# A two-layer encoder trunk on one NeuronCore: operands of the inner groups of hidden columns split one product sooner, the order at the end of the channel mixer changed, the last 256 hidden columns turned by VectorE and DMA, two constant tiles made in place

## The chip, the cores and the metric

The kernel runs on one core of one Trainium2 chip. The metric is the device time of one execution in microseconds. Before the change it was 931.45 us, the median of three runs (931.14, 931.45 and 932.04 us).

## The reference, cut to what matters

Two layers over 256 tokens of width 1024. Each layer runs a SwiGLU channel mixer with half weight, an attention block (a windowed and a differential head group), and a second SwiGLU mixer; a last RMSNorm follows. All of it is float32. The change touches the channel mixer, which runs four times, and the constants of the attention.

```python
D_MODEL, SEQ, DEPTH, D_FF = 1024, 256, 2, 2816

def swiglu(h, w_gate, w_up, w_down):
    return (jax.nn.silu(h @ w_gate) * (h @ w_up)) @ w_down

for l in range(DEPTH):
    x = x + 0.5 * swiglu(rms_norm(x, ffn1_norm[l]), ffn1_w_gate[l], ffn1_w_up[l], ffn1_w_down[l])
    x = x + attention_block(x, l)        # uses lam = exp(sum(lam_q1*lam_k1)) - exp(sum(lam_q2*lam_k2)) + lam_init
    x = x + 0.5 * swiglu(rms_norm(x, ffn2_norm[l]), ffn2_w_gate[l], ffn2_w_up[l], ffn2_w_down[l])
return rms_norm(x, final_norm)
```

## The kernel before, in words

**Products.** A float32 product is made of three TensorE matmuls on a faster float32 form: each operand is split into a high part (a rounding copy by ScalarE) and a low part (a subtraction by VectorE), and high x high, low x high and high x low are accumulated in PSUM. For weights this splitting is `emit_split` (L205): one ACT `CAST w<-raw` and one DVE `TENSOR_TENSOR w<-raw,w` for each half of a 1 MB weight tile. `weights()` (L262) is called ahead of every product; through `ahead` (L241) it first writes down the splits, and the loads that SyncE issues, of the products that come next, up to six halves further on. 14 `w` buffers (seven halves) and 6 `raw` buffers hold them, so the split of a half waits until TensorE has let go of the half seven places before.

**Groups.** The 2816 hidden columns are five groups of 512 (0 to 4) and a last group of 256. Groups 0, 1 and 3 are plain: gate and up, four products of 24 matmuls each (`Plain`, L691). Groups 2 and 4 use a seven-product scheme over the two token tiles and the two halves of the depth (`Seven`, L642): parts a, d, ab, c, abc, bc, abcd with 12 matmuls each; its weight sums are partly made by accumulating DMAs on GpSimd's queue (`gather`, L154), and `abcd` is the last part of a group. The last 256 columns have gate and up side by side in one tile and take two products of 24 matmuls (`last`, first and second half of the depth).

**Turning.** The hidden values come out with tokens on the partitions; the down projection needs the hidden columns there. For groups 0 to 4 `Flip` (L719) does this without TensorE: two DVE stream transposes (32x32 blocks) into one buffer, then eight DMAs on SyncE's queue (L727) that carry the blocks to their partitions. `Flip.operands` (L729), called at "turned" in the order, splits the result into high and low parts: two ACT casts and two DVE subtractions on `s` tiles (`s<-s`). For the last 256 columns `turn` (L707) uses four TensorE transposes with the identity and one split out of PSUM.

**Order.** `order()` (L34) is a list by hand, walked in `ffn` (L763), and each engine executes its instructions in the order in which they are written down. "flip" starts group 1's or 3's `Flip` (groups 0, 2 and 4 start it on their own when their last product is done), "turned" splits its result, "down" g, h is group g's share of the output columns h (24 matmuls, written d0_0 to d4_1 below). "aside" is `attention_constants` (L517) in the first mixer. After the list, `ffn` splits group 4's operands (L785) and computes the last group's hidden values (L786); `ffn_end` (L792) runs three quarters of d4_0, calls the deferred `turn` (L806), and then the last quarter. `tail` multiplies the last 256 columns.

In the second half of one mixer the order before is, for TensorE: ... abc, 3, bc, 3, abcd, 3, 3 (parts of group 2 and products of group 3 in turn), a, d1_0, d, d1_1, ab, d2_0, c, d2_1, abc, last 0, bc, d3_0, abcd, last 1, d3_1, d4_0 with the transposes in it, then d4_1 and the tail.

**Buffers.** The `s4` pool has 14 buffers of 4 KB per partition for operands, hidden values and flips. Two of them hold constants from the start of the kernel until "aside" in the first mixer: `dist_i` (an iota) and `lams` (the four lambda vectors and their products).

Of the kernel before, what the change touches and what calls it, by code (L numbers as in the profile page):

```python
# [9 lines left out]
F32 = mybir.dt.float32  # L10
F32R = mybir.dt.float32r
AF = mybir.ActivationFunctionType
ALU = mybir.AluOpType

P = 128
D = 1024
S = 256
DEPTH = 2
# [3 lines left out]
NGRP = FF // 512  # L22
# [11 lines left out]
def order():  # L34

    two, four = [[("seven", g, p) for p in ("a", "d", "ab", "c", "abc", "bc", "abcd")] for g in (2, 4)]
    one, three = [[("plain", g, (w, k0)) for w in range(2) for k0 in (0, 4)] for g in (1, 3)]
    downs = [[("down", g, h) for h in range(2)] for g in range(4)]
    last = [("last", 0, k0) for k0 in (0, 4)]
    sums = [("sums", 0, 1)]  # L40
    turn = [[("turned", g, 0)] for g in range(4)]
    flip = [[("flip", g, 0)] for g in range(4)]
    aside = [("aside", 0, 0)]

    def weave(a, b):
        out = []
        for i in range(max(len(a), len(b))):
            out += a[i:i + 1] + b[i:i + 1]
        return out

    seq = sums + one[:1] + sums + two[:1] + sums + one[1:2] + sums + two[1:2] + turn[0] + one[2:]
    seq += two[2:3] + flip[1] + downs[0][:1] + two[3:4] + downs[0][1:]
    seq += weave(two[4:], three) + flip[3] + turn[1]
    seq += four[:1] + downs[1][:1] + four[1:2] + turn[2] + downs[1][1:] + four[2:3] + downs[2][:1] + four[3:4] + turn[3] + downs[2][1:] + four[4:5]
    seq += last[:1] + four[5:6] + downs[3][:1] + four[6:] + last[1:] + aside + downs[3][1:]
    return seq


# [5 lines left out]
def trunk(ctx: ExitStack, tc: tile.TileContext, x, n1, g1, u1, d1, nm, w_in, sink,  # L64
# [4 lines left out]
    class Kept:  # L69


        def __init__(self, eng):
            self.eng = eng
# [26 lines left out]
    def bank():  # L100
        return ps.tile([P, 512], F32, tag="ps", bufs=8, name=nm_("ps"))

    def halves(b):
        return b.rearrange("p (a n) -> p a n", a=2)

    def blk(dt=F32R):
        return s4.tile([P, 2, 512], dt, tag="s4", name=nm_("s4"))
# [379 lines left out]
    slopeB = [2.0 ** -(2 * (h + 1)) for h in range(4)]  # L487
    lam_init = [0.8 - 0.6 * math.exp(-0.3 * l) for l in range(DEPTH)]

    dist_i = s4.tile([P, 2, S], mybir.dt.int32, tag="s4", name="dist_i")  # L490
    lams = blk(F32)
    lin = lams[:, 0].rearrange("p (i d) -> p i d", i=4)
    lpr = lams[:, 1, 0:2 * DEPTH * 64].rearrange("p (i d) -> p i d", i=2)
    def constants():
        for i, g in enumerate((nm, n2)):
            pool.dma_start(grow[i * 16:(i + 1) * 16], g.rearrange("l (k p) -> (l k) p", p=P))
        pool.dma_start(grow[32:34], subln)
        pool.dma_start(snk_in, sink.rearrange("l h -> (l h)").partition_broadcast(P))
        for i, a in enumerate((lq1, lk1, lq2, lk2)):
            pool.dma_start(lin[:, i], a.rearrange("l d -> (l d)").partition_broadcast(P))  # L500
        pool.iota(dist_i.rearrange("p a b -> p (a b)"), pattern=[[P, 2], [-1, S]], base=0, channel_multiplier=1)

        for c in range(4):
            pool.memset(qscA[0:64, c:c + 1], -0.125 / slopeA[c])
            pool.memset(qscA[64:128, c:c + 1], -0.125 / slopeA[c + 4])
            pool.memset(qscB[:, c:c + 1], -0.125 / slopeB[c])

        sv = snk_in.rearrange("p (l s c) -> p l c s", l=DEPTH, s=2)
        for t in range(2):
            for l in range(DEPTH):  # L510
                pool.tensor_copy(snk[:, l, :, t, :], sv[:, l])
        pool.tensor_scalar(nsnk.rearrange("p a b c d -> p (a b c d)"), snk.rearrange("p a b c d -> p (a b c d)"),
                           -1.0, 0.0, op0=ALU.mult, op1=ALU.add)
        for i in range(2):
            pool.tensor_tensor(lpr[:, i], lin[:, 2 * i], lin[:, 2 * i + 1], op=ALU.mult)

    def attention_constants():  # L517
        gsl = bank()
        pe.transpose(gsl[:, 0:NG - 16], grow, ident[:NG - 16, :NG - 16])
        dve.tensor_copy(gcol[:, 16:NG], gsl[:, 0:NG - 16])  # L520
        dflat = distB.rearrange("p a b -> p (a b)")
        aflat = distA.rearrange("p a b -> p (a b)")
        dve.tensor_copy(aflat, dist_i.rearrange("p a b -> p (a b)"))
        dve.scalar_tensor_tensor(dflat, in0=aflat, scalar=-1.0, in1=aflat, op0=ALU.mult, op1=ALU.max)
        dve.tensor_scalar(aflat, dflat, 128.5, BIG, op0=ALU.is_gt, op1=ALU.mult)
        dve.tensor_tensor(aflat, aflat, dflat, op=ALU.add)
        dve.tensor_reduce(lsum.rearrange("p a b -> p (a b)"),
                          lpr.rearrange("p a (l d) -> p (a l) d", l=DEPTH), axis=mybir.AxisListType.X, op=ALU.add)
        lex = const.tile([P, 2, DEPTH], F32, name="lex")
        act.activation(lex, lsum, AF.Exp)  # L530
        dve.tensor_tensor(nlam, lex[:, 1], lex[:, 0], op=ALU.subtract)
        for l in range(DEPTH):
            dve.tensor_scalar_add(nlam[:, l:l + 1], nlam[:, l:l + 1], -lam_init[l])
            dve.tensor_scalar_mul(gsub[:, l:l + 1], gcol[:, 48 + l:49 + l], 1.0 - lam_init[l])
# [13 lines left out]
    def split(dst, src, scale=None):  # L548

        act.copy(dst[:, :, 0:S], src)  # L550
        dve.tensor_tensor(dst[:, :, S:512], src, f(dst[:, :, 0:S]), op=ALU.subtract)
# [57 lines left out]
    def ffn(norm, aside=None, before=None, final=False):  # L609
# [4 lines left out]
        def gate(gs):  # L614
            g = []
            for t in range(2):
                n = gs[t].shape[1]
                g.append(silu(tmp().rearrange("p a n -> p (a n)")[:, :n], gs[t], t))
            return g
# [5 lines left out]
        def hidden(g, us):  # L625
            h = blk(F32)
            for t in range(2):
                up(h, us[t], g[t], t)
            return h
# [12 lines left out]
        class Seven:  # L642


            def __init__(self, g):
                self.g = g
# [57 lines left out]
                    hid[self.g] = hidden(self.gate, self.acc)  # L704
                    self.gate = self.acc = None

        def turn(hs, n):  # L707
            out_ = []
            for i in range(n):
                sl = halves(bank())  # L710
                for c in range(2):
                    for t in range(2):
                        pe.transpose(sl[:, c, t * P:(t + 1) * P], hs[:, t, (2 * i + c) * P:(2 * i + c + 1) * P], ident)
                hb = blk()
                split(hb, sl)
                out_.append(hb)
            return out_

        class Flip:  # L719


            def __init__(self, h):
                sq, self.back = blk(F32), blk(F32)
                for t in range(2):
                    dve.transpose(sq[:, t].rearrange("p (g m) -> p g m", g=4), h[:, t].rearrange("p (c i g) -> p g c i", c=4, g=4))
                    for b in range(4):
                        sp.dma_start(self.back[:, t, b * P:(b + 1) * P], sq[32 * b:32 * b + 32, t])  # L727

            def operands(self):  # L729

                out_ = []
                for i in range(2):
                    hb = blk()
                    src = self.back.rearrange("p t (b c j) -> p c (t b) j", b=4, c=4)[:, 2 * i:2 * i + 2]
                    hi, lo = [hb[:, :, a:a + S].rearrange("p c (y j) -> p c y j", j=32) for a in (0, S)]
                    act.copy(hi, src)
                    dve.tensor_tensor(lo, src, f(hi), op=ALU.subtract)
                    out_.append(hb)
                return out_
# [23 lines left out]
        for what, n, part in ORDER:  # L763
# [17 lines left out]
            elif what == "last":  # L781
                if part == 0:
                    gu = [bank(), bank()]
                tokens(gu, norm.xs, weights(), part)
        hT = hid.pop(NGRP - 1).operands()  # L785
        h = hidden(gate([b[:, 0:256] for b in gu]), [b[:, 256:512] for b in gu])  # L786
        return accs, hT, lambda: turn(h, 1)

    BY_TOKENS = [(k, t) for t in range(2) for k in range(2)]
    G4 = 4 * (NGRP - 1)  # L790
# [1 line left out]
    def ffn_end(parts, last):  # L792

        accs, hT, rest = parts
        hT = [None] * (2 * (NGRP - 1)) + hT
        hE = []
        w = {0: weights()}

        def group(h, order, a=None, c=slice(None), first=0):
            tokens(a or accs[h], hT, w[h], G4, first=first, last=last[h], order=order, cols=c)  # L800

        def tail(h, order=BY_TOKENS, a=None, c=slice(None)):
            tokens(a or accs[h], [None] * (2 * NGRP) + hE, w["rest"], 4 * NGRP, last=last[h], order=order, cols=c, h=h)

        group(0, [(k, t) for k in range(3) for t in range(2)])
        hE.extend(rest())  # L806
        group(0, [(3, t) for t in range(2)])
        w["rest"] = weights()
        w[1] = weights(2)
        return group, tail  # L810
# [337 lines left out]
```

## Time and profile before

| quantity | value |
|---|---|
| median of three runs | 931.45 us |
| the profiled execution, device time | 930.48 us |
| its span, first to last instruction | 928.7 us |
| TensorE matmuls busy | 914.0 us, 98% of the span |
| VectorE busy | 708.2 us, 76% |
| ScalarE busy | 558.7 us, 60% |
| GpSimd busy | 52.7 us, 6% |
| granted TensorE clock, mean | 0.999 |
| DMA | 205.10 MB, mean 221 GB/s |

A row of the timeline reads: start in us, duration in us, engine, line, operation, output and inputs, form, number of merged instructions, and in brackets the idle time of the engine before it with what ended that. PE is TensorE, DVE is VectorE, ACT is ScalarE, POOL is GpSimd, SPq is SyncE's queue. The program's tiles are `w` (split weights), `raw` (weights as loaded), `s` (the `s4` pool), `q` and `v` (sums for the seven-product scheme), `ps` (PSUM). Most instructions carry L79, the line of a recording helper, so they are told apart by their tiles and their place in time. Matmuls overlap, so the duration of a row is longer than the distance from its start to the next row's start; the pace of TensorE is read from starts.

### The profile page before, as it was taken

How to read it: one execution, taken by the hardware profiler on the slowest of the kernel's cores; microseconds unless marked ns; L12 is line 12 of the kernel's file. 1: busy time of each engine (PE TensorE's matmuls, PEld its weight loads, DVE VectorE, ACT ScalarE, POOL GpSimd, SP SyncE). 2: the span in 40 equal slices, each digit the busy share in tenths (PEclk: the TensorE clock that was granted, in tenths of full speed). 3: DMA queues.
4: the chain of work that ended last, by engine and by line, in shares of the span. 5: the costliest groups of instructions: out<-in, count | busy, mean ns of one | idle time of the engine just before them, and what ended most of it. 6: DMA issues, size and time to landing. Idle time of an engine off the chain costs nothing.

```text
span 928.7 us, 12908 instructions
## 1 busy us (share of the span) xinstructions
PE 914.0 (98%) x4684; PEld 772.4 (83%) x4684; DVE 708.2 (76%) x998; ACT 558.7 (60%) x869; POOL 52.7 (6%) x73
## 2 busy tenths in 40 slices
PE   8999999999999999999999999999999999999997
PEld 6878788799898888788888887888999888887886
DVE  6688987778956788887668978876796658978873
ACT  7665665567735665565475655555685475656552
POOL 0400010000000000010000100000000000100001
PEclk9999999999999999999999999999999999999999
DMA  9979999645424879999648899986642448899921
GB/s 339 307 214 335 298 251 330 187 174 140 137 90 135 249 197 324 261 253 306 211 170 245 217 312 244 291 272 198 180 150 91 135 140 246 213 317 262 274 92 46
DMA packets 133936, 205.10 MB, mean 221 GB/s; under 512 B 6126, under 2 KB 54320, under 8 KB 133872
## 3 DMA queue, kind: packets, MB, share of 16 engines
q1 hardware_dynamic: 119856, 177.76, 57.9%
q0 software_dynamic: 12928, 25.46, 16.0%
q10 hardware_dynamic: 1088, 1.05, 0.4%
q8 instruction: 37, 0.61, 0.3%
q14 instruction: 27, 0.22, 0.1%
HBM read 192.71 MB, written 1.05 MB: 209 GB/s over the span
## 4 chain that ended last, share of the span: by engine, by line
PE 91%; SPq 2%; DVE 2%; DMA 1%; issue 1%; ACT 1%; ACTq 0%; POOLq 0%; POOL 0%; DVEq 0%
PE ps L79 91%; SPq L727 2%; DVE s L79 1%; DMA s<-s 1%; ACT w L79 1%; DVE w L79 1%; DMA xk<-in_x_dram 0%; ACT tmp L79 0%; ACT s L79 0%; DVE xk L79 0%; DVE tmp L79 0%; ACTq L79 0%; POOLq L1143 0%; POOL rf L79 0%; DVE rf L79 0%
## 5 line engine op out<-in xcount | busy, mean ns | idle before, releaser
L79 PE MATMUL ps<-w,s 128*128 128x512 f32 (+1 forms) x2994 | 692.6, 390 | 4.1 <-DVE s L79 3.1
L79 PEld LDWEIGHTS ps<-w,s 128*128 128x128 f32 x2994 | 557.1, 188 | 123.2 <-DVE s L79 6.1
L79 DVE TENSOR_TENSOR w<-raw,w 128x1024 fp32r<-128x1024 f32 (+1 forms) x416 | 437.4, 1088 | 121.9 <-ACT w L79 118.6
L79 ACT CAST w<-raw 128x1024 fp32r<-128x1024 f32 (+1 forms) x416 | 377.9, 943 | 220.6 <-PE ps L79 151.6
L79 PE MATMUL ps<-s,w 128*128 128x256 f32 x672 | 84.0, 285 | 0.0
L79 PEld LDWEIGHTS ps<-s,w 128*128 128x128 f32 x672 | 81.7, 192 | 1.1
L79 PE MATMUL ps<-w,q 128*128 128x512 f32 x288 | 69.2, 389 | 0.0
L79 PEld LDWEIGHTS ps<-w,q 128*128 128x128 f32 x288 | 54.1, 188 | 11.2
L79 ACT ACTIVATE s<-ps,gcol 128x256 fp32r<-128x256 f32 (+1 forms) x80 | 31.3, 477 | 20.6 <-PE ps L79 20.6
L79 DVE STREAM_TRANSPOSE s<-s 128x512 f32<-128x512 f32 x40 | 41.5, 1075 | 0.0
L79 POOL DMA_DIRECT2D raw<-in_ffn_w_up_dram x16 | 20.7, 1297 | 297.0 <-DVE w L79 126.2
L79 ACT ACTIVATE s<-s,negm 128x256 f32<-128x256 f32 x64 | 31.9, 500 | 6.5 <-DVE negm L79 6.5
L79 ACT CAST q<-tmp 128x512 fp32r<-128x512 f32 x20 | 12.4, 620 | 38.8 <-DVE tmp L79 38.8
L79 DVE TENSOR_TENSOR s<-s,s 128x512 fp32r<-128x512 f32 x40 | 25.7, 683 | 10.7 <-ACT s L79 10.7
L79 DVE SCALAR_TENSOR_TENSOR s<-ps,gcol,s 128x256 fp32r<-128x256 f32 x48 | 20.3, 478 | 14.4 <-ACT s L79 14.3
L79 ACT ACTIVATE tmp<-ps,r 128x512 f32<-128x512 f32 (+1 forms) x40 | 24.3, 641 | 6.4 <-PE ps L79 5.8
L79 ACT CAST s<-s 128x512 fp32r<-128x512 f32 x40 | 22.6, 613 | 1.4 <-DMA s<-s 1.4
L79 PE MATMUL ps<-w,v 128*128 128x512 f32 x96 | 23.1, 389 | 0.0
L79 POOL TENSOR_TENSOR r<-ms,mhalf 128x2 f32<-128x2 f32 x6 | 4.3, 710 | 300.6 <-DVE ms L79 300.6
L79 DVE TENSOR_TENSOR tmp<-tmp,ps 128x512 f32<-128x512 f32 x24 | 16.5, 686 | 6.3 <-PE ps L79 6.3
L79 PEld LDWEIGHTS ps<-w,v 128*128 128x128 f32 x96 | 18.0, 188 | 3.7
L79 DVE SCALAR_TENSOR_TENSOR s<-ps,hr,tmp 128x512 f32<-128x512 f32 (+1 forms) x32 | 20.5, 679 | 0.2 <-ACT tmp L79 0.2
(110 smaller groups left out, 427.7 us busy)
## 6 DMA issues: line engine op xcount, KB each, us to landing
raw<-in_ffn_w_down_dram SPq DMA_DIRECT2D x44, 1024.0 KB, 7.3
raw<-in_ffn_w_gate_dram SPq DMA_DIRECT2D x39, 1024.0 KB, 6.0
raw<-in_ffn_w_up_dram SPq DMA_DIRECT2D x39, 1024.0 KB, 5.4
raw<-in_ffn_w_up_dram POOLq DMA_DIRECT2D x16, 1024.0 KB, 8.8
raw<-in_w_in_dram SPq DMA_DIRECT2D x14, 1024.0 KB, 5.5
s<-s SPq DMA_DIRECT2D x160, 64.0 KB, 4.3
raw<-in_ffn_w_gate_dram POOLq DMA_DIRECT2D x8, 1024.0 KB, 11.8
raw<-in_ffn_w_gate_dram SPq DMA_DIRECT2D x8, 512.0 KB, 6.3
```

The lines of the kernel that those rows point to most:

```text
L79: ins = issue(*a, **k)
L727: sp.dma_start(self.back[:, t, b * P:(b + 1) * P], sq[32 * b:32 * b + 32, t])
```

## The change

The order list gets two more "turned" entries (groups 4 and 5) and is rearranged. Group 1's operands are split behind the second product of group 3, three products sooner; group 2's ahead of part d, one product sooner; group 3's behind abc. Then come d2_1, bc, last 0, abcd, last 1, "aside", d3_0, group 4's split, d3_1 and the split of the last 256 columns. So d3_0 moves from between bc and abcd to behind last 1, abc moves ahead of d2_1, and all of d3 stands between the last hidden product and d4. `Flip` takes a width; the last 256 columns (called group 5) go through it as soon as their second product is done: two DVE transposes of 256 columns and eight DMAs in place of four TensorE transposes. `turn` is gone. `dist_i` becomes a view of `distA` and the lambda vectors a view of `distB`, so the two `s4` buffers are free; the sum of the lambda products is taken ahead of the distances that overwrite it.

```diff
-    turn = [[("turned", g, 0)] for g in range(4)]
+    turn = [[("turned", g, 0)] for g in range(6)]
...
-    seq += weave(two[4:], three) + flip[3] + turn[1]
-    seq += four[:1] + downs[1][:1] + four[1:2] + turn[2] + downs[1][1:] + four[2:3] + downs[2][:1] + four[3:4] + turn[3] + downs[2][1:] + four[4:5]
-    seq += last[:1] + four[5:6] + downs[3][:1] + four[6:] + last[1:] + aside + downs[3][1:]
+    seq += weave(two[4:6], three[:2]) + turn[1] + two[6:] + three[2:] + flip[3]
+    seq += four[:1] + downs[1][:1] + turn[2] + four[1:2] + downs[1][1:] + four[2:3] + downs[2][:1] + four[3:5] + turn[3] + downs[2][1:]
+    seq += four[5:6] + last[:1] + four[6:] + last[1:] + aside + downs[3][:1] + turn[4] + downs[3][1:] + turn[5]
...
-    dist_i = s4.tile([P, 2, S], mybir.dt.int32, tag="s4", name="dist_i")
-    lams = blk(F32)
-    lin = lams[:, 0].rearrange("p (i d) -> p i d", i=4)
-    lpr = lams[:, 1, 0:2 * DEPTH * 64].rearrange("p (i d) -> p i d", i=2)
+    dist_i = distA.bitcast(mybir.dt.int32)
+    lin = distB.rearrange("p a (i d) -> p (a i) d", d=DEPTH * 64)
+    lpr = lin.rearrange("p (a i) d -> p a i d", i=2)[:, :, 0]
...
-            pool.tensor_tensor(lpr[:, i], lin[:, 2 * i], lin[:, 2 * i + 1], op=ALU.mult)
+            pool.tensor_tensor(lpr[:, i], lpr[:, i], lin[:, 2 * i + 1], op=ALU.mult)
...
+        dve.tensor_reduce(lsum, lpr.rearrange("p a (l d) -> p a l d", l=DEPTH), axis=mybir.AxisListType.X, op=ALU.add)
...
-        dve.tensor_reduce(lsum.rearrange("p a b -> p (a b)"),
-                          lpr.rearrange("p a (l d) -> p (a l) d", l=DEPTH), axis=mybir.AxisListType.X, op=ALU.add)
...
-        def turn(hs, n):
...
-            def __init__(self, h):
-                sq, self.back = blk(F32), blk(F32)
+            def __init__(self, h, n=512):
+                self.n, m = n, n // 4
+                sq, back = [blk(F32).rearrange("p a n -> p (a n)")[:, :2 * n].rearrange("p (t n) -> p t n", t=2) for _ in range(2)]
+                self.back = back
                 for t in range(2):
-                    dve.transpose(sq[:, t].rearrange("p (g m) -> p g m", g=4), h[:, t].rearrange("p (c i g) -> p g c i", c=4, g=4))
+                    dve.transpose(sq[:, t].rearrange("p (g m) -> p g m", g=4), h[:, t, :n].rearrange("p (c i g) -> p g c i", i=32, g=4))
                     for b in range(4):
-                        sp.dma_start(self.back[:, t, b * P:(b + 1) * P], sq[32 * b:32 * b + 32, t])
+                        sp.dma_start(back[:, t, b * m:(b + 1) * m], sq[32 * b:32 * b + 32, t])
...
-                for i in range(2):
+                for i in range(self.n // 256):
...
                 tokens(gu, norm.xs, weights(), part)
-        hT = hid.pop(NGRP - 1).operands()
-        h = hidden(gate([b[:, 0:256] for b in gu]), [b[:, 256:512] for b in gu])
-        return accs, hT, lambda: turn(h, 1)
+                if part:
+                    hid[NGRP] = Flip(hidden(gate([b[:, 0:256] for b in gu]), [b[:, 256:512] for b in gu]), 256)
+                    gu = None
+        return accs, hT[NGRP - 1], hT[NGRP]
...
-        hE.extend(rest())
+        hE.extend(rest)
```

More of the change, by code (lines that the diff above doesn't have):

```diff
@@ L705, in part @@
                     self.gate = self.acc = None
-        def turn(hs, n):
[L708 to L717, printed above, removed]
         class Flip:
-            def __init__(self, h):
-                sq, self.back = blk(F32), blk(F32)
+            def __init__(self, h, n=512):
+                self.n, m = n, n // 4
+                sq, back = [blk(F32).rearrange("p a n -> p (a n)")[:, :2 * n].rearrange("p (t n) -> p t n", t=2) for _ in range(2)]
+                self.back = back
                 for t in range(2):
-                    dve.transpose(sq[:, t].rearrange("p (g m) -> p g m", g=4), h[:, t].rearrange("p (c i g) -> p g c i", c=4, g=4))
+                    dve.transpose(sq[:, t].rearrange("p (g m) -> p g m", g=4), h[:, t, :n].rearrange("p (c i g) -> p g c i", i=32, g=4))
                     for b in range(4):
-                        sp.dma_start(self.back[:, t, b * P:(b + 1) * P], sq[32 * b:32 * b + 32, t])
+                        sp.dma_start(back[:, t, b * m:(b + 1) * m], sq[32 * b:32 * b + 32, t])
             def operands(self):
                 out_ = []
-                for i in range(2):
+                for i in range(self.n // 256):
                     hb = blk()
-                    src = self.back.rearrange("p t (b c j) -> p c (t b) j", b=4, c=4)[:, 2 * i:2 * i + 2]
+                    src = self.back.rearrange("p t (b c j) -> p c (t b) j", b=4, j=32)[:, 2 * i:2 * i + 2]
                     hi, lo = [hb[:, :, a:a + S].rearrange("p c (y j) -> p c y j", j=32) for a in (0, S)]
```

## The prediction

> **What bounds the kernel now.** First the page's head, then the chain that ended last and the waits, to see which engine sets the end.
>
> ```profile
> span 928.7 us, 12908 instructions
> PE 914.0 (98%) x4684; PEld 772.4 (83%) x4684; DVE 708.2 (76%) x998; ACT 558.7 (60%) x869; POOL 52.7 (6%) x73
> by line: PE ps L79 91.5%; SPq L727 2.2%; DVE s L79 1.3%; issue 1.2%; DMA s<-s 1.0%; ACT w L79 0.6%; DVE w L79 0.5%; DMA xk<-in_x_dram 0.4%; ACT tmp L79 0.2%; ACT s L79 0.1%; DVE xk L79 0.1%; DVE tmp L79 0.1%; ACTq L79 0.1%; POOLq L1143 0.1%
> ACT w L79 <- PE ps L79: 151.6, 136, 3.9
> PE ps L79 <- DVE s L79: 3.1, 6, 1.0
> ```
>
> TensorE is busy 98% of the span and carries 91.5% of the chain. ScalarE waits 151.6 us for TensorE to free weight buffers, so the splits run ahead. What can be won is TensorE's own work and its few stalls; the only repeated one is six waits for VectorE on an `s` tile. The flip DMAs (L727) in the chain feed it. So I read the timeline of TensorE alone, mixer by mixer, and take its pace from starts.
>
> ```profile
> 366.69 22.15 PE L79 MATMUL ps<-w,s 128*128 128x512 f32 x97
> 389.31 13.67 PE L79 MATMUL ps<-w,s 128*128 128x512 f32 x59 [0.47 <-DVE s L79]
> 402.81 2.88 PE L79 MATMUL ps<-w,q 128*128 128x512 f32 x12
> 405.53 5.60 PE L79 MATMUL ps<-w,s 128*128 128x512 f32 x24
> ...
> 109.44 13.69 PE L79 MATMUL ps<-w,s 128*128 128x512 f32 x59 [0.47 <-DVE s L79]
> ...
> 566.94 13.67 PE L79 MATMUL ps<-w,s 128*128 128x512 f32 x59 [0.46 <-DVE s L79]
> ...
> 845.04 13.71 PE L79 MATMUL ps<-w,s 128*128 128x512 f32 x59 [0.47 <-DVE s L79]
> ```
>
> Pace: 405.53 - 402.81 = 2.72 us for 12 matmuls, 0.2267 each; a product of 24 takes 5.44. The 97 from 366.69 should end at 388.68; the next starts at 389.31, 0.63 late. The 59 after it take 13.50 where 13.37 are due, 0.12 more (the start after a stall is rough). The place is the second matmul of d1_0, and all four mixers have the same row, so 0.74 each.
>
> ```profile
> 164.03 6.09 PE L79 MATMUL ps<-w,s 128*128 128x512 f32 x25
> 171.16 4.15 PE L79 MATMUL ps<-w,s 128*128 128x512 f32 x17 [1.03 <-DVE s L79]
> 175.15 0.60 PE L79 MATMUL ps<-ident,s 128*128 128x128 f32 x4
> 175.50 9.82 PE L79 MATMUL ps<-w,s 128*128 128x512 f32 x42
> ...
> 430.01 19.44 PE L79 MATMUL ps<-w,s 128*128 128x512 f32 x85
> 449.65 4.16 PE L79 MATMUL ps<-w,s 128*128 128x512 f32 x17 [0.20 <-DVE s L79]
> 453.65 0.60 PE L79 MATMUL ps<-ident,s 128*128 128x128 f32 x4
> 454.01 9.79 PE L79 MATMUL ps<-w,s 128*128 128x512 f32 x42
> 463.64 1.03 PE L79 MATMUL ps<-ident,xk 128*128 128x128 f32 x8
> ...
> 630.91 0.60 PE L79 MATMUL ps<-ident,s 128*128 128x128 f32 x4
> ```
>
> The second place is the second matmul of d4_0. Second mixer: 430.01 + 85 x 0.2267 = 449.28, start 449.65, 0.37 late, and the 17 after it take 4.00 for 3.85: 0.49 or so (0.37 and 0.12). First mixer: 171.16 - (164.03 + 5.67) = 1.46 and 0.14, less 0.2 for the restart behind the small transpose ahead of 164.03, which stays: 1.4. The third and fourth have none. Then the four transposes: 0.36 us from 453.65 to 454.01, and the 42 matmuls behind take 0.11 more than 9.52: 0.45 in each mixer.
>
> **The change part by part.** *Group 1's operands sooner.* Why VectorE is late at d1_0:
>
> ```profile
> 378.06 8.01 SPq L727 DMA_DIRECT2D s<-s  x8
> 383.94 1.14 ACT L79 CAST s<-s 128x512 fp32r<-128x512 f32 x2
> 385.25 1.43 DVE L79 SCALAR_TENSOR_TENSOR s<-ps,hr,tmp 128x512 f32<-128x512 f32 x2
> 386.60 2.08 DVE L79 STREAM_TRANSPOSE s<-s 128x512 f32<-128x512 f32 x2
> 388.60 1.25 DVE L79 TENSOR_TENSOR s<-s,s 128x512 fp32r<-128x512 f32 x2
> ```
>
> ScalarE had its half at 385.1. VectorE's two subtractions stand behind group 3's two multiplications, which need group 3's last product, and its two transposes; they start at 388.60 and TensorE goes at 389.31. Group 1's flip was long done. In the new order they stand three products (12 + 24 + 24 matmuls, 13.6 us) sooner; 1.14 us of ScalarE and 1.25 us of VectorE move and none are added. What is late next is group 2's flip, by at most 1.3 us; its split is due at d2_0, whose first matmul is that at 405.53, over 17 us behind the end of its DMA issues (378.06 + 8.01), and they land 2 to 8 us later (below). Saved: 4 x 0.74 = 2.96 us. Bounds: 0, if something else in VectorE's queue holds d1_0, and 2.96; I take 2.96, as the row behind the stall is this one.
>
> *d3_0 behind last 1.* Group 4's last product ends, in the second mixer, at 430.01 + 36 x 0.2267 = 438.17.
>
> ```profile
> 440.91 5.47 SPq L727 DMA_DIRECT2D s<-s  x8
> 448.25 1.14 ACT L79 CAST s<-s 128x512 fp32r<-128x512 f32 x2 [0.90 <-DMA s<-s]
> ...
> 170.41 1.29 DVE L79 TENSOR_TENSOR s<-s,s 128x512 fp32r<-128x512 f32 x2
> ```
>
> From 438.17 to 449.65 are 11.5 us (flip issue from +2.7 to +8.2, landing, cast, subtraction); in the first mixer the same from 158.3 (150.17 + 36 x 0.2267, row below) to 171.16, 12.8. The cover was two products, 10.9 us; it becomes three, 16.3. So 1.4 + 0.49 = 1.9 us go, with 3.5 us to spare. In the first mixer two ACT table loads stand in that stretch (before and behind the lambda's Exp); the silu of the last columns now comes ahead of the Exp and one of them falls away, off TensorE's path. Bounds 0 and 1.9; I take 1.9.
>
> *abc and abcd come one product sooner.* The wait at risk is the sum that GpSimd's accumulating DMA brings for abcd:
>
> ```profile
> 407.74 2.21 ACT L79 CAST w<-raw 128x1024 fp32r<-128x1024 f32 x2 [1.41 <-DVE raw L79]
> 419.13 2.88 PE L79 MATMUL ps<-w,q 128*128 128x512 f32 x12
> ...
> 131.66 1.28 POOL L79 DMA_DIRECT2D raw<-in_ffn_w_gate_dram  x1 [6.05 <-DVE w L79]
> 146.14 5.05 ACT L79 CAST w<-raw 128x1024 fp32r<-128x1024 f32 x5 [4.47 <-DMA raw<-in_ffn_w_gate_dram]
> 150.17 13.76 PE L79 MATMUL ps<-w,s 128*128 128x512 f32 x60
> ```
>
> It is issued when abc is split, and abc is now split sooner too. Were it not to move, abcd would be due in the first mixer at 150.17 + 5.44 - 5.44 - 0.74 = 149.4 and be cast from 146.14; behind two casts of 1.01 (5.05/5), a subtraction as wide as the two of 388.60 (1.25) and one of half that width that clears the PSUM bank (0.63) it could go at 150.0: 0.6 us lost there. I take 0, and 0.6 for the range. abc itself was cast at 407.74 for a product that starts at 419.13 (the second mixer), 9 us ahead, so the 5.4 are covered.
>
> *The last 256 columns.* Out go 16 TensorE transposes: 4 x 0.45 = 1.78 us. In come, per mixer, two DVE transposes and eight DMAs; cast and subtraction stay.
>
> ```profile
> L79 DVE STREAM_TRANSPOSE s<-s 128x512 f32<-128x512 f32 x40 | 41.5, 1075 | 0.0
> L79 DVE SCALAR_TENSOR_TENSOR s<-ps,hr,tmp 128x256 f32<-128x256 f32 x8 | 3.5, 478 | 0.2 <-ACT tmp L79 0.2
> L727 SPq DMA_DIRECT2D s<-s x160: 542/602/2268, 38.2 to 901.2; - x160
> DMA to landing us min/median/max: 2.1/4.3/8.3
> 387.93 8.67 SPq L727 DMA_DIRECT2D s<-s  x8
> ```
>
> A 256-wide transpose is not in the trace: between 0.48 (another 256-wide operation) and 1.08 (the 512-wide one); I take 0.54, half. Counted from the end of last 1: group 4's eight issues run until +2.8 (8.2 - 5.4), the new eight at 0.60 until +7.6, landing 4.3 later at +11.9, cast and subtraction 1.3: +13.2. The tail needs it 78 matmuls on (d3_0, d3_1, d4_0 and six), at +17.7. So it lies beside matmuls, with 4.5 us to spare. Behind the eight on SyncE's queue stand weight loads, some 5 us later than now; behind the cast and the subtraction, which wait for the DMAs, stand splits on ScalarE and VectorE, which run ahead (the 151.6 above). Cost 0; from the other side both sets of eight at the widest 8.67 and the latest landing of 8.3: issues from -2.7 to +6.0 and +14.6, landed +22.9, ready +24.2, 6.5 us late in each mixer.
>
> Here the Trainium skill speaks against the change: VectorE: DVE Perf Modes, The three transpose paths and Rules for kernel authors, has a full 128x128 transpose done on TensorE, as VectorE turns only 32x32 blocks. By that rule the 1.78 would stay in and the sum be 4.9; the trace has 1.1 us of VectorE time beside 76% busy against 0.45 us on the engine at 98%, so I go by the rows.
>
> *Constants in place.* Two `s4` buffers come free; no TensorE wait in the trace is for an `s4` buffer of the first mixer, so 0. The `s` tiles waited for above are late results, not buffers.
>
> *Sum:* 2.96 + 1.9 + 1.78 = 6.6 us. The profiled execution of 930.48 (span 928.7 and 1.8 around it) becomes 923.8; the median of the runs lies 1.0 above it, so 931.45 becomes **924.8 us**.
>
> **The rivals.** A: *d1_0 still stalls*, for its weights or another late VectorE result. For it: VectorE has the same work in the same stretch; against: the split of d1_0's weights is older than the operand split that is waited for. Without 2.96: 927.8. With abcd's 0.6 as well, 928.4.
>
> B: *no change*: the stalls turn up at the next wait, at d2_0 and in the tail, and the queue behind eight more DMAs takes back the transposes' time. 931.4. Against it: 17, 3.5 and 4.5 us of cover.
>
> C: *slower: the last columns come back late.* The place is the first tail matmul, the price what the eight added DMAs and the two operand splits behind them lack. Its far end is 4 x 6.5 = 26 us, 950.8; it makes the kernel slower than before once the operands are ready later than +17.7 + 6.6/4 = +19.4. Half way between that point and the far end, at +21.8, it costs 4.1 a mixer: 941. For it: landings up to 8.3 and issues up to 2.27 us each stand in the row; against: at the end of a mixer (440.91) eight took 5.47, with few loads in flight.
>
> **How the numbers follow.** Forecast 0.72 (923.6 to 926, abcd's 0.6 and some 0.5 between runs, 931.14 to 932.04, within it), A 0.15 (926 to 928.4), B 0.06, C 0.07. Range 923.2 to 928.4: the forecast and nearly all of A. No change means within 0.2%, 1.9 us, about what a measurement of this kernel can tell: 929.6 to 933.3. Faster 0.87, same 0.06, slower 0.07.
>
> **What would show it.** Right: the wait of PE `ps` for DVE `s` loses its 0.46 to 0.47 rows and the 1.03; the rows of four `ps<-ident,s` in d4_0 are gone and the 42 matmuls join the 17; PE busy is lower by some 2 us while DVE gains 4; L727 has 192 issues. A: a bracket remains on the second matmul of d1_0. B or C: a bracket naming DVE `s` or ACT `s` stands in the tail, behind 30 matmuls of d4, with a landing of `s<-s` over 6 us before it. Wrong altogether: a stall in the early products of the next mixer from loads behind the eight DMAs.

## The result and the profile after

| | before | after |
|---|---|---|
| median, four runs each, compared together | 931.75 us (931.14 to 932.64) | 923.59 us (923.26 to 924.47) |
| the profiled execution, device time | 930.48 us | 923.26 us |
| its span | 928.7 us | 921.5 us |

The ratio is 0.9913, 95% interval 0.9896 to 0.993, which is 6.5 to 9.7 us less. The profiled executions differ by 7.2 us, the medians by 8.2. In a later comparison the changed kernel took 923.4 (five runs) against 930.97, 7.6 less. The forecast was 6.6 less than before, 924.8.

The head of the changed kernel's page and its chain of waits:

```profile
span 921.5 us, 12949 instructions
PE 909.5 (99%) x4668; PEld 771.8 (84%) x4668; DVE 710.8 (77%) x1006; ACT 553.4 (60%) x867; POOL 52.9 (6%) x73
PE 98%; DMA 0%; issue 0%; DVE 0%; ACT 0%; POOLq 0%; POOL 0%; ACTq 0%; DVEq 0%
```

TensorE carries 98% of the chain that ended last, and the flip DMAs, 2.2% of it before, have left. TensorE has sixteen matmul instructions fewer, the transposes. The view of what each engine waited for (total us, times, longest), one of ScalarE's rows and all of TensorE's:

```profile
ACT s L79 <- DMA s<-s: 14.8, 8, 3.6
PE ps L79 <- DMA grow<-in_ffn_norm_dram: 3.4, 1, 3.4
PE ps L79 <- DMA xk<-in_x_dram: 0.7, 2, 0.4
PE ps L79 <- DVE w L79: 0.5, 1, 0.5
PE ps L79 <- ACT w L79: 0.2, 1, 0.2
```

The wait of TensorE for a VectorE result on an `s` tile, before six waits of 3.1 us in total, has no row. In its place ScalarE waits 14.8 us for landings of `s<-s`, and no row has TensorE waiting for ScalarE's `s`: the splits of groups 4 and 5 now stand ready before their data, and not the other way round. TensorE's timeline at the old stalls, first the stretch that holds d1_0 of the second mixer, then d4_0 of the second and of the first (the view's window can cut a row, so it need not begin or end with a product):

```profile
363.50 31.67 PE L79 MATMUL ps<-w,s 128*128 128x512 f32 x139
...
427.65 24.64 PE L79 MATMUL ps<-w,s 128*128 128x512 f32 x108
...
159.74 20.56 PE L79 MATMUL ps<-w,s 128*128 128x512 f32 x90
```

139 matmuls at 0.2267 us are 31.5 us, 108 are 24.5, 90 are 20.4; each row is that long and one overlap more, so no bracket and no transpose is left inside. Group 1's split and what feeds the second row, on VectorE:

```profile
370.37 1.29 DVE L79 TENSOR_TENSOR s<-s,s 128x512 fp32r<-128x512 f32 x2 [1.39 <-ACT s L79]
...
440.86 1.29 DVE L79 TENSOR_TENSOR s<-s,s 128x512 fp32r<-128x512 f32 x2 [1.63 <-DMA s<-s]
446.37 0.69 DVE L79 TENSOR_TENSOR s<-s,s 128x512 fp32r<-128x512 f32 x1 [1.68 <-ACT s L79]
```

Group 1's operands are done at 371.7 for a product that starts at 385.3 (the 96 matmuls from 363.50). Group 4's are done at 442.15, and d4_0's second matmul starts at 445.3. The last columns' are done at 447.06. The second mixer's last hidden product ended 29 matmuls into the second row, at 427.65 + 29 x 0.2267 = 434.2, so that is +12.8 where the prediction has +13.2, and the tail needs them at +17.7.

The rows of the new pieces, from the groups by form, the view of the DMA issues' line and the page:

```profile
L79 DVE STREAM_TRANSPOSE s<-s 128x256 f32<-128x256 f32 x8 | 4.6, 617 | 0.0
...
L715 SPq DMA_DIRECT2D s<-s x192: 542/602/2149, 38.2 to 894.7; - x192
...
s<-s SPq DMA_DIRECT2D x160, 64.0 KB, 4.9
```

A 256-wide transpose takes 0.62 us (0.54 taken), an issue 0.60 as the 160 before. The 160 DMAs of 64 KB, those of the groups of 512, take 4.9 us to land by the median, where the page of before has 4.3. The kernel with d3 moved alone, which has none of the 32 new DMAs, shows 4.9 too.

### The profile page after: what moved, and what is told of

The parts are those of the page before. It is cut to its first block, busy times and chain, and to the rows that moved or that the text cites. A ratio compares the mean times of both kernels' runs of the same rounds, so it can differ in the third digit from the quotient of the medians.

```text
span 921.5 us, 12949 instructions
## 1 busy us (share of the span) xinstructions
PE 909.5 (99%) x4668; PEld 771.8 (84%) x4668; DVE 710.8 (77%) x1006; ACT 553.4 (60%) x867; POOL 52.9 (6%) x73
## 4 chain that ended last, share of the span: by engine, by line
PE 98%; DMA 0%; issue 0%; DVE 0%; ACT 0%; POOLq 0%; POOL 0%; ACTq 0%; DVEq 0%
PE ps L79 98%; DMA xk<-in_x_dram 0%; DVE w L79 0%; ACT w L79 0%; DVE s L79 0%; ACT tmp L79 0%; DVE xk L79 0%; ACT s L79 0%; POOLq L1132 0%; POOL rf L79 0%; ACTq L79 0%; DVE rf L79 0%; DVEq L79 0%
## 5 line engine op out<-in xcount | busy, mean ns | idle before, releaser
L79 DVE STREAM_TRANSPOSE s<-s 128x512 f32<-128x512 f32 (+1 forms) x48 | 46.1, 1000 | 0.0
L79 DVE TENSOR_TENSOR s<-s,s 128x512 fp32r<-128x512 f32 x44 | 28.6, 687 | 19.2 <-ACT s L79 17.6
L79 ACT CAST s<-s 128x512 fp32r<-128x512 f32 x44 | 25.1, 615 | 14.8 <-DMA s<-s 14.8
L79 DVE TENSOR_TENSOR q<-tmp,q 128x512 fp32r<-128x512 f32 x20 | 13.8, 691 | 8.2 <-ACT q L79 8.2
```

Source lines behind the costliest of these rows:

```text
L79: ins = issue(*a, **k)
```

## The experiments

Each part was first made alone on the kernel before. These four share one comparison, in which the kernel before had a median of 931.07 us (26 runs).

**Group 1's operands sooner, alone.**

```diff
-    seq += weave(two[4:], three) + flip[3] + turn[1]
+    seq += weave(two[4:6], three[:2]) + turn[1] + two[6:] + three[2:] + flip[3]
```

> The kernel before with one edit: group 1's operands are split three products sooner, all else as it was. Theory (three separate terms that add up): the stall at the second matmul of d1_0 goes in all four mixers, 4 x 0.74 = 2.9 us, so some 928.8 us against 931.75, and in the trace the four waits of 0.46 to 0.47 us on a DVE s tile are gone while those at d4_0 (1.03 and 0.20) and the 16 transposes of the last columns stay. Rival A (something else in VectorE's queue holds d1_0): a bracket stays on the second matmul of d1_0 and the time stays within 0.5 us of 931.75.

927.64 us, ratio 0.9967 (0.9955 to 0.9979): 3.4 us by the medians, 2.0 to 4.2 by the interval. Group 1's split stands three products sooner; the one product of the title is group 2's. TensorE's row over d1_0 of the second mixer has no bracket any more, and of the six waits for VectorE's `s` the two at d4_0 are left:

```profile
385.83 16.48 PE L79 MATMUL ps<-w,s 128*128 128x512 f32 x72
...
PE ps L79 <- DVE s L79: 1.3, 2, 1.0
```

The step holds, with its 2.96 inside the interval.

**d3 behind the last hidden product, alone** (group 1's and group 2's splits where they were, the TensorE transposes kept).

```diff
-    seq += four[:1] + ... + four[3:4] + turn[3] + downs[2][1:] + four[4:5]
-    seq += last[:1] + four[5:6] + downs[3][:1] + four[6:] + last[1:] + aside + downs[3][1:]
+    seq += four[:1] + ... + four[3:5] + turn[3] + downs[2][1:]
+    seq += four[5:6] + last[:1] + four[6:] + last[1:] + aside + downs[3][:1] + turn[4] + downs[3][1:]
```

> The kernel before with the new order from group 4 on (abc ahead of d2_1, d3_0 behind the second last-columns product, group 4's operands split ahead of d3_1), the last columns still turned by TensorE, group 1's and 2's operands split where they were. Theory: the d4_0 waits (1.03 and 0.20 us as the profile sees them, 1.4 and 0.5 by the pace) go, 1.9 us, so some 929.9 us; the four d1_0 waits stay. Rival (the stall only moves to the next wait): a new wait of 0.5 us or more at d3_0, d3_1 or the tail, and 931 us or more.

928.46 us, ratio 0.9972 (0.9962 to 0.9982), 2.6 us less by the medians, 1.7 to 3.5 by the interval. d4_0 of the first and second mixer, and TensorE's waits for VectorE's `s`:

```profile
159.81 14.46 PE L79 MATMUL ps<-w,s 128*128 128x512 f32 x63
...
445.77 6.51 PE L79 MATMUL ps<-w,s 128*128 128x512 f32 x28
...
PE ps L79 <- DVE s L79: 1.9, 4, 0.5
```

The matmuls run unbroken, the transposes stand behind each row, and the four waits left are those at d1_0. The 1.9 that one execution of before had shown is inside the interval. That place is not the same in every trace: in that of the kernel with group 1's part alone (929.91 us, the longest of its six executions), whose order here is the old one, the second mixer reads

```profile
445.67 3.56 PE L79 MATMUL ps<-w,s 128*128 128x512 f32 x15
449.94 0.50 PE L79 MATMUL ps<-w,s 128*128 128x512 f32 x1 [0.71 <-ACT s L79]
450.67 4.15 PE L79 MATMUL ps<-w,s 128*128 128x512 f32 x17 [0.22 <-DVE s L79]
```

By the pace the first bracket's start is 0.87 us late (449.94 for 445.67 + 15 x 0.2267) and the second's 0.50, 1.4 in all where the prediction's row gave 0.37 (0.49 with its slow restart). By the same count it is 0.65 and 0.82 in the two traces, further down, whose order here is the old one and which differ from before by the lambda's sum and the constants.

**The last 256 columns through VectorE and DMA, alone, in the old order.** The edit is that of the change (`Flip` with a width, `turn` gone), with one line of the order:

```diff
-    seq += last[:1] + four[5:6] + downs[3][:1] + four[6:] + last[1:] + aside + downs[3][1:]
+    seq += last[:1] + four[5:6] + downs[3][:1] + four[6:] + last[1:] + aside + downs[3][1:] + turn[4] + turn[5]
```

> The kernel before with only the last 256 columns turned by VectorE and DMA, split behind group 4's operands; the order of products as it was. Here the operands are due 54 matmuls (12.2 us) behind the last hidden product and not 78 (17.7 us). Theory (the transposes' 1.78 us are a term of their own, and the moved d3 is the cover): the DMAs come back at about the time they are due: gain between 1.8 us (no wait) and 0 (a wait of 0.4 us in each mixer), 930 to 931.7, with a wait on an s tile in the tail or none. Rival C (the last columns come back late, at 13.2 us by the estimate or later): a wait of 1 us or more at the first tail matmul in every mixer, 934 us or more.

931.56 us, ratio 1.0011 (1.0002 to 1.002): no gain, by the interval a loss of 0.2 to 1.9 us. The time is inside the range expected, but not for the cause named: no wait stands in the tail. The transposes are gone, and in the profiled execution (932.12 us) more than their time is lost at d4_0 of the first mixer. TensorE there, then ScalarE and SyncE:

```profile
163.71 5.73 PE L79 MATMUL ps<-w,s 128*128 128x512 f32 x24
171.09 0.50 PE L79 MATMUL ps<-w,s 128*128 128x512 f32 x1 [1.65 <-ACT s L79]
172.62 9.60 PE L79 MATMUL ps<-w,s 128*128 128x512 f32 x34 [1.03 <-DVE s L79]
...
168.43 0.21 ACT L79 ACTIVATE lex<-lsum 128x4 f32<-128x4 f32 x1 [3.01 <-DVE lsum L79]
...
170.42 1.14 ACT L79 CAST s<-s 128x512 fp32r<-128x512 f32 x2
...
160.74 12.04 SPq L717 DMA_DIRECT2D s<-s  x16
```

Group 4's copies (170.42) stand on ScalarE behind the lambda's Exp, which waits 3.01 us for VectorE's `lsum`. TensorE loses 3.1 us by its pace, where the kernel before lost 1.4, and then 34 matmuls take 9.60 us instead of 7.9: the section on the hardware returns to that.

**The constants in place, alone.** The edit is that part of the change, with the sum of the lambda products ahead of the four distance operations.

> The kernel before with only the two constant tiles made in place. Theory: no wait of TensorE is for these buffers, 931.75 within 0.5 us, and the stall of 0.45 us ahead of abcd of group 2 in the first mixer, which is gone in the changed kernel, stays as it was or moves with the landing of the accumulating DMA. Rival: the two free buffers take that stall away, and perhaps part of the ones at 61 and 62 us: 0.4 us or more faster.

929.97 us, ratio 0.9991 (0.9982 to 0.9999), 1.1 us less: the rival's time. VectorE and ScalarE in the first mixer, first in the kernel before, then in this one, with group 4's subtractions, the last columns' multiplications behind them, and TensorE's row at d4_0:

```profile
166.51 0.41 DVE L79 TENSOR_REDUCE lsum<-s 128x4 f32<-128x256 f32 x1
...
166.96 0.20 ACT L79 ACTIVATE lex<-lsum 128x4 f32<-128x4 f32 x1 [3.58 <-DVE lsum L79]
```

```profile
164.32 0.42 DVE L79 TENSOR_REDUCE lsum<-distB 128x4 f32<-128x256 f32 x1
...
164.77 0.21 ACT L79 ACTIVATE lex<-lsum 128x4 f32<-128x4 f32 x1 [1.33 <-DVE lsum L79]
...
169.61 1.28 DVE L79 TENSOR_TENSOR s<-s,s 128x512 fp32r<-128x512 f32 x2
170.91 0.88 DVE L79 SCALAR_TENSOR_TENSOR s<-ps,hr,tmp 128x256 f32<-128x256 f32 x2
...
170.35 4.16 PE L79 MATMUL ps<-w,s 128*128 128x512 f32 x17 [0.29 <-DVE s L79]
```

The sum is 2.2 us sooner, the Exp follows it at once, and TensorE's bracket at d4_0 falls from 1.03 to 0.29. Whether the moved line does this or the two freed buffers, the next four runs tell; they share a comparison with 931.02 us for the kernel before (21 runs).

**One line moved.** The kernel before, tiles untouched, with the sum ahead of the four distance operations.

```diff
         dve.tensor_copy(gcol[:, 16:NG], gsl[:, 0:NG - 16])
+        dve.tensor_reduce(lsum..., lpr..., axis=mybir.AxisListType.X, op=ALU.add)
...
         dve.tensor_tensor(aflat, aflat, dflat, op=ALU.add)
-        dve.tensor_reduce(lsum..., lpr..., axis=mybir.AxisListType.X, op=ALU.add)
```

> The kernel before with one line moved: the sum for the lambda in front of the four distance operations on VectorE; tiles and all else as before. Theory (this move is what the in-place constants gain at d4_0 of the first mixer): the wait for DVE s there falls from 1.3 to about 0.45 us, the Exp starts some 2.2 us sooner, time 930.2, ratio 0.9991. Rival (the freed buffers do it): time as before, 931.07 within 0.4, and the wait of 1.3 still there.

929.94 us, ratio 0.9988 (0.9979 to 0.9997), as with all of the constants' part. Its Exp starts at 164.78, and its row at d4_0 is the same:

```profile
170.35 4.15 PE L79 MATMUL ps<-w,s 128*128 128x512 f32 x17 [0.29 <-DVE s L79]
```

The moved line alone gives the whole gain; the freed buffers show none. So the rival above had the time and not the cause.

**The changed kernel with the old constants.** The constants' part of the diff is undone, the sum behind the distances again.

> The changed kernel with the constants in s4 buffers and an operand tile, and the sum for the lambda behind the four distance operations again. Theory (its gain comes from the lambda's Exp, which ScalarE runs ahead of group 4's splits: 2.2 us earlier with the change; three products of cover hide it either way): the Exp is back 2.2 us behind, no wait at d4_0 of the first mixer, time 923.6 within 0.5. Rival (in-place constants bring their 1.1 us here too, through the accumulating DMA for abcd of group 2 or another way): 924.3 to 924.7, and a row of 0.2 to 0.9 with DVE tmp at abcd of group 2 in the first mixer.

922.87 us (922.52 to 923.1), ratio 0.9913 (0.9899 to 0.9926). Beside the other parts the constants show no gain. ScalarE and VectorE in the first mixer:

```profile
161.70 0.21 ACT L79 ACTIVATE lex<-lsum 128x4 f32<-128x4 f32 x1 [3.01 <-DVE lsum L79]
...
163.99 1.14 ACT L79 CAST s<-s 128x512 fp32r<-128x512 f32 x2 [0.19 <-DMA s<-s]
...
165.16 1.29 DVE L79 TENSOR_TENSOR s<-s,s 128x512 fp32r<-128x512 f32 x2
```

The Exp again waits 3.01 us, but group 4's operands are done at 166.45, and d4_0's second matmul starts at 168.2, the fiftieth of the row that starts at 156.99: 1.8 us are left of the cover that d3 gives, where the changed kernel's profile has 2.6 (165.94 and 168.58).

**The changed kernel with TensorE's transposes.** The last 256 columns as before, in the new order.

```diff
-    seq += four[5:6] + last[:1] + four[6:] + last[1:] + aside + downs[3][:1] + turn[4] + downs[3][1:] + turn[5]
+    seq += four[5:6] + last[:1] + four[6:] + last[1:] + aside + downs[3][:1] + turn[4] + downs[3][1:]
```

> The changed kernel with the last 256 columns turned by TensorE again: 16 transposes instead of the DVE transposes and the 32 small DMAs, at the same place of the order. Theory (with group 4's last product as cover, the other route costs nothing): 1.78 us are lost, 923.6 becomes 925.4, ratio to before about 0.993, and four rows of four transposes of 128x128 stand in d4_0 of each mixer. Rival, from the run that made this one edit alone and gained nothing: the transposes' 1.78 is taken back elsewhere, and the time stays at 923.6 within 0.5.

924.69 us, ratio 0.9934 (0.9921 to 0.9946). That is 1.8 over the kernel with the old constants beside it, and 1.3 over the changed kernel's 923.4 in the other comparison. The intervals of the ratios overlap, so the direct times alone do not settle the size. The trace shows where it goes, here in the second mixer:

```profile
449.72 0.60 PE L79 MATMUL ps<-ident,s 128*128 128x128 f32 x4
450.08 6.16 PE L79 MATMUL ps<-w,s 128*128 128x512 f32 x26
```

0.36 us from start to start, and 6.16 for 26 matmuls that take 6.05 with their overlap: the 0.45 of the prediction, which the new order with VectorE's route does not have.

**Columns through VectorE and the constants in place, in the old order.** The two edits above together.

> The kernel before with two parts: the last 256 columns through VectorE and the DMAs, and the constants in place. The former alone gave 1.0011 of the time before; its trace has 1.78 us less of transposes, but 3.3 us of waits at d4_0 of the first mixer, where it was 1.3. Theory (that loss is the Exp of the lambda, now behind the last columns' two activations and in front of group 4's splits): with the sum 2.2 us earlier it shrinks by about 2, and the time becomes 929.3 to 929.8, ratio 0.998 to 0.9987. Rival (it is the sixteen DMA issues in one row that hold up the splits): the wait of about 3 stays and the time is 931 or more less the 0.45 at abcd at most.

932.25 us (929.63 to 933.49), ratio 1.0008 (0.9999 to 1.0017), so the theory fell in its number, and the time is the rival's. The trace is that of its shortest execution, 929.63 us: there the Exp is sooner and the wait smaller, though by less than 1 us (2.12 in one bracket for 1.65 and 1.03 in two). TensorE, ScalarE and VectorE in the first mixer:

```profile
171.45 10.76 PE L79 MATMUL ps<-w,s 128*128 128x512 f32 x46 [2.12 <-DVE s L79]
...
165.87 0.21 ACT L79 ACTIVATE lex<-lsum 128x4 f32<-128x4 f32 x1 [0.79 <-DVE lsum L79]
...
167.87 1.14 ACT L79 CAST s<-s 128x512 fp32r<-128x512 f32 x2
...
163.51 0.86 DVE L79 SCALAR_TENSOR_TENSOR s<-ps,hr,tmp 128x256 f32<-128x256 f32 x2
164.30 1.13 DVE L79 STREAM_TRANSPOSE s<-s 128x256 f32<-128x256 f32 x2
...
170.71 1.28 DVE L79 TENSOR_TENSOR s<-s,s 128x512 fp32r<-128x512 f32 x2
```

The data had landed and the copies stood at 167.87; what TensorE waits for is VectorE, whose subtractions for group 4 begin at 170.71. In front of them stand the last columns' multiplications and transposes, 1.9 us from 163.51 to 165.4, which with the constants alone come behind group 4's split (170.91 behind 169.61). The wait grew by as much, from 0.29 to 2.12. So in this execution the rival's sixteen issues are not it, and the Exp is only a part: the flip of the last columns puts its own work in front of group 4's split, and in the old order only two products cover that. What the median execution, 2.6 us longer, loses more is not in this trace; the section on the hardware returns to it.

**A stall that is left.** In the changed kernel TensorE still waits at d0_0 of the first mixer:

```profile
60.93 0.73 PE L79 MATMUL ps<-w,s 128*128 128x512 f32 x2 [0.24 <-ACT w L79]
62.19 5.29 PE L79 MATMUL ps<-w,s 128*128 128x512 f32 x22 [0.52 <-DVE w L79]
```

One run moved a sum that stands there, another repeated the changed kernel; both with 930.97 us for the kernel before (9 runs).

```diff
-    seq = sums + one[:1] + sums + two[:1] + sums + one[1:2] + sums + two[1:2] + turn[0] + one[2:]
+    seq = sums + one[:1] + sums + two[:1] + sums + one[1:2] + two[1:2] + turn[0] + one[2:3] + sums + one[3:]
```

> The changed kernel with the fourth partial sum of the norm moved behind the next product of the first mixer's opening (sums, one[1:2], two[1:2], turn[0], one[2:3], sums, one[3:]). In the changed kernel's trace ScalarE idles 2.1 us there for VectorE's tmp with the casts of d0_0's weights queued behind, and TensorE waits 0.24 + 0.52 us for these weights at d0_0, 1.3 us by its pace. Theory (that order is the cause): the two rows at d0_0 go and the time falls by up to 1.3 us below the changed kernel's. Rival (the weights' landing is the cause, or the sum's later place makes abc late instead): the rows stay, or turn up at the next product, and the time is that of the changed kernel within 0.4.

923.62 us, ratio 0.9927 (0.9913 to 0.994): no gain. The rows at d0_0 are gone and the wait turns up at the seven-product part after it, for VectorE's half of that part's weights:

```profile
75.32 2.58 PE L79 MATMUL ps<-w,q 128*128 128x512 f32 x10 [0.60 <-DVE w L79]
```

> The changed kernel itself, beside the next one on the same chip. Theory (its gain is 2.96 + 1.9 + 1.78 = 6.6 us on the path, and 0.45 more in those executions of the kernel before in which the accumulating DMA for abcd of group 2 lands late): 923.2 to 924.4, ratio 0.9915 to 0.9925. Rival (the in-place constants cost something, since the kernel without them took 922.87): the median lies 0.5 or more above that.

923.4 us (923.2 to 924.27), ratio 0.9923 (0.991 to 0.9935). Beside this the kernel with the old constants, 922.87, cannot be told from it, and no version tried is shown to beat the changed kernel. The profiled execution, 924.27 us, has a wait that the first profile of after did not have. TensorE at abcd of group 2 in the first mixer, then the accumulating DMA and the cast that follows its landing:

```profile
92.69 3.68 PE L79 MATMUL ps<-w,s 128*128 128x512 f32 x15 [0.59 <-DVE tmp L79]
...
76.11 1.27 POOL L79 DMA_DIRECT2D raw<-in_ffn_w_gate_dram  x1 [13.84 <-DVE w L79]
...
87.37 5.79 ACT L79 CAST w<-raw 128x1024 fp32r<-128x1024 f32 x6 [8.98 <-DMA raw<-in_ffn_w_gate_dram]
```

11.3 us lie from that issue to the cast. In the first profile of after it was 9.8 (the rows below), and there was no wait:

```profile
75.96 1.27 POOL L79 DMA_DIRECT2D raw<-in_ffn_w_gate_dram  x1 [15.46 <-DVE w L79]
...
85.75 5.80 ACT L79 CAST w<-raw 128x1024 fp32r<-128x1024 f32 x6 [7.49 <-DMA raw<-in_ffn_w_gate_dram]
```

The kernel before had 10.9 in its profile (75.97 to 86.85) and waited, 0.45 us by the pace; that kernel with one line moved, the same up to there, had 10.1 (76.53 to 86.59) and did not wait. So this wait comes and goes between executions in either kernel, and is not the change's.

## Why the prediction was right, point by point

*Group 1's operands (2.96).* Shown: alone it gave 3.4 us (2.0 to 4.2), and the four rows are gone. Group 2's earlier split was not run alone; the changed kernel has no wait at d2_0.

*d3_0 behind last 1 (1.9).* Shown: alone it gave 2.6 (1.7 to 3.5). That 1.9 is too small is not shown by the times, but the traces point that way: the working took the second mixer's lateness from one execution, and that is the smallest of the four traces of the old order above. The 3.5 us to spare are those of the first mixer; for the second the same sum gives 16.3 - 11.5 = 4.8. TensorE can go on with the first of group 4's two subtractions (0.69 us each), so 3.2 were left in the first mixer (165.35 against 168.58) and 3.8 in the second (441.55 against 445.33). In the second that subtraction ended 12.8 us behind group 4's last product, where the working has 11.5, and ScalarE waited 2.23 us for the landings ahead of it. In the two traces with the same order and TensorE's transposes (d3 alone, and the changed kernel with them) it is 11.1. Whether the eight new DMAs delay those landings is not shown.

*The last columns (1.78).* The transposes' 0.45 each is what the trace shows, and the route beside the matmuls cost nothing, as long as d3 stands in front of it: in the old order the same edit gained nothing. The prediction costed the eight DMAs against the tail, where the last columns are due, which is rival C's place. It did not cost what the new transposes and activations put in front of group 4's split on VectorE and ScalarE; that is where it bit when the cover was gone. By the Trainium skill's rule that a full transpose belongs on TensorE (VectorE: DVE Perf Modes, Rules for kernel authors) the 1.78 would have stayed in. The run with TensorE's transposes shows the opposite here: 0.45 us in each mixer on the engine that sets the end, against VectorE time that TensorE does not wait for.

*Constants in place (0).* Right in the change, and for a reason that the working lacks. It looked at the buffers, which gave nothing; the moved sum is worth 1.1 us alone, and d3's cover hides it.

*abcd (0, bounded by 0.6).* Right: the term is about group 4, and neither trace of the changed kernel has a wait at its abcd. The wait that comes and goes stands at abcd of group 2, whose place in TensorE's order the change leaves alone and which the working does not name. In the two profiled executions it favoured the later one by some 0.45 us, so of the 7.2 us between them about 6.7 are the change.

*The sum.* 6.6 was forecast. Two parts made alone give 3.4 + 2.6 and the third, taken out again, 1.3 to 1.8: 7.3 to 7.8, and the whole 7.6 to 8.2 by the medians, 6.1 to 9.7 by the two intervals. The 6.6 is inside, near the low end. Rivals A, B and C did not occur: no bracket at d1_0, and none in the tail. Two of the signs named came out in another size: TensorE's busy time fell by 4.5 us and not by some 2, and VectorE's rose by 2.6 and not by 4. What may be low in the sum is the size at d4_0, and the way from one execution to the median: the kernel before lay 1.0 above its profiled execution, the changed one 0.3. That waits which vary between executions were in that 1.0 and left with the change is argued, not shown. One sign of it: the executions of the changed kernel lie within 1.3 us of one another in either comparison, the 26 of the kernel before within 3.9, though so many more would spread wider in any case.

## What to carry to other kernels

Work taken off the bounding engine is only gained if the detour is covered where it ends and also where its instructions stand in front of other results: count what the new pieces push back in each queue, and not only their own due time. An order that lengthens the cover and an edit that needs cover belong together; tried singly the second looks worthless. When a buffer trick forces an instruction to another place, look at the place first: here one reduction in front of four element-wise operations was the whole effect.

## What the runs showed of the hardware

In one trace a pause of TensorE cost more than itself. With the last columns turned in the old order, the 2.7 us of waits with one matmul between them (brackets of 1.65 and 1.03) were followed by half clock. One window of that kernel (in us, the busy times of the engines, then TensorE's granted clock, the DMA share and GB/s):

```profile
173.00:176.00 3.00, 3.00 (x8) 2.32 (x8) 1.08 (x3) 1.57 (x2) 0.00 (x0) 0.50 0.65 147
```

and the same window of the one with the constants in place as well, after its single wait of 2.12 us:

```profile
173.00:176.00 3.00, 3.00 (x15) 2.47 (x14) 2.42 (x3) 1.71 (x2) 0.00 (x0) 1.00 1.08 365
```

Eight matmuls against fifteen in the same 3 us: at 0.2267 us each that is some 1.6 us more. In no other stretch of the twelve traces does TensorE work at a lowered clock. The Trainium skill (TensorE: Matmul & The Clock Gate, Part 1) describes a halving of the clock after an idle window of about 3.4 us. Here 2.7 us with a matmul in it were followed by the halving and 2.12 us were not; both are below that figure, and two cases give no threshold.

That the scatter of the second kernel comes from the same halving is argued, not shown. Of its eleven executions, the seven with a mean granted clock of 0.996 or 0.997 took 931.7 to 933.5 us; of the four with 0.998 or 0.999, three took 929.6 to 930.6 and one 932.3. The mean alone is no proof, because it also counts the time behind the last matmul, where a low clock costs nothing: the profile of after has a mean of 0.997, and its clock is lowered only there (0.60 from 916 to 920 us, with the last matmul's end at 914.5).
